# A hybrid GLA + S5 decoder block: S5 steps and gate matrix loaded beside the prologue, VectorE and ScalarE in one written order up to S5

## The chip, the core and the metric

The kernel runs on one core of a Trainium2 chip. The core has five engines that run side by side: TensorE (matrix products, PE in the profile), VectorE (DVE), ScalarE (ACT), GpSimd (POOL) and SyncE (SP, which here only issues transfers). The metric is the device time of one execution in microseconds (us); lower is better.

## The reference, cut to what matters

528 tokens (16 meta tokens and 512 of the sequence) of width 1024 go through one decoder block in fp32:

```
xn   = rmsnorm(h, g_mix_pre)
proj = xn @ w_in               # q, k, v, r, a_low, u, z_gla, z_ssm
log_a = log_sigmoid(a_low @ w_gate_up + b_gate) / 16      # decay of each GLA channel
o    = gla_chunked(q, k, v, log_a);  y_gla = (rmsnorm(o) * silu(r)) @ w_o_gla
y_s  = s5_ssm(u, ...)          # complex diagonal recurrence, 64 groups x 64 states
y_ssm = GLU(gelu(y_s) @ w_glu + b_glu)
mixed = sigmoid(z_gla) * y_gla + sigmoid(z_ssm) * y_ssm
h    = h + rmsnorm(mixed @ w_out);  h = h + rmsnorm(relu(rmsnorm(h) @ w_ff1)**2 @ w_ff2)
```

The S5 part needs, before any token is seen, a short calculation on 64 x 64 parameters: a step `exp(log_step)`, the complex factor `lam = exp(a * step)` (an exponential, a sine and a cosine), its powers 0 to 8, the eighth power normalised and its own powers (E8), and the matrices B and C scaled with these.

## The kernel before, in words

Every large product runs as three passes on a split of both operands into a high half and a rest (`mm3`, `feat_tile`): `whi` and `wlo` are the halves of a weight tile of 128 columns, `xh` and `xl` those of the normalised tokens. A weight tile is loaded to `wraw` (three buffers) on SP's queue, ScalarE makes `whi` (`split_w_hi`) and VectorE `wlo` (`split_w_lo`). One such product of 512 columns is a slot: `dense` is the list of slots, `slot()` runs one, and `fetch` splits weights two slots ahead (`AHEAD = 2`).

The kernel begins with a prologue. The first five tiles of `u` are multiplied with the unnormalised tokens (`rh`, `rl`; `raw_product`), while ScalarE squares the token rows (`squared`), `rooted` makes the reciprocal root of the mean square (`xrs`; token tiles 0 and 1 first, then 2 to 4), and `spread` and `rows_of` turn it into rows (`xrows`, `xrowp`). `scaled`, `high` and `low` then make the normalised tokens (`xT`, `xh`, `xl`) for two halves of the tokens. `u_took(..., raw=True)` takes a raw product out of PSUM into `ut`, multiplied with `xrowp`; `u_out` stores it on POOL's queue. `wa` is the split weight of the gate's low rank (`a_low`).

Then come the low-rank product (`low_rank`, result `alow`), and ten slots: three tiles of `u`, four gate tiles of z_ssm (zs0 to zs3) and three of z_gla (zg4 to zg6). Between them stand the gate products (`gate_up`, which need the split gate matrix `wgr`), the decay sums (`decay_sums`, exp, log and a scan), the S5 steps (`chain`, `powers`, `b_bar`, `chunk_powers`, `c_rows`), and the tables of S5's first block (`first`). Behind the ten slots the loop over the heads and S5's blocks begins with a product of 256 columns.

What sets the order: TensorE runs in program order through all of this (`pinned`). In the prologue VectorE and ScalarE are wrapped in `InOrder`, which keeps program order; from `V, S = nc.vector, nc.scalar` on a scheduler places their instructions. Transfers run in the order of the queue they are issued on (SP, POOL, ScalarE). In this kernel the gate matrix `wgu` is loaded with six transfers and the S5 steps and parameters `ab` with one, all on POOL's queue.

## Time and profile before

| | us |
|---|---|
| median of 3 runs | 891.54 |
| lowest and highest run | 888.96, 893.45 |
| profiled execution, its own time | 893.47 |
| its span in the profile | 891.8 |
| TensorE busy | 870.5 (98%) |
| VectorE busy | 651.7 (73%) |
| ScalarE busy | 445.6 (50%) |
| GpSimd busy | 125.3 (14%) |

The profile is one execution, with times from the start of its span. Rows name an instruction by engine, line, operation and tiles (out<-in). A row of the timeline has the start, the duration and in brackets the idle time before it and what ended that. A row of the stretches has the stretch, its length, busy time of each engine with the number of instructions, the granted TensorE clock (1.00 is full), the busy share of the transfer engines and what they moved in GB/s. With a filter for one engine only that engine's busy time is shown. In the waits a row has the waiting engine, line and tile, what it waited for, the sum, the number of times and the longest.

### The profile page before, as it was taken

To read this page: it belongs to the slowest core of one execution; us is meant where nothing else is said; L and a number is where in the kernel's file an instruction comes from. 1 tells how busy PE (TensorE), PEld (TensorE's weight loads), DVE (VectorE), ACT (ScalarE), POOL (GpSimd) and SP (SyncE) were. 2 spreads that over 40 slices of the span, in tenths; PEclk is the share of its full clock that TensorE was granted. 3 is DMA by queue.
4 is the path that set the end of the run, shared out by engine and by line. 5 is a ranking of instruction groups with operands and counts; after the bars stand their busy time and mean duration, and the time that the engine had idled before them with its cause. 6 is when DMAs were issued, how large, how long until landed. Compare 5 with 4: busy or idle time off the path is not lost.

```text
span 891.8 us, 13281 instructions
## 1 busy us (share of the span) xinstructions
PE 870.5 (98%) x4824; PEld 744.1 (83%) x4824; DVE 651.7 (73%) x1180; ACT 445.6 (50%) x751; POOL 125.3 (14%) x220
## 2 busy tenths in 40 slices
PE   9789899999999999999999999999999999999996
PEld 8778698989898888888888888988888888888885
DVE  5778979787786869966544765576667668688886
ACT  7549355676665545425333543433222236665763
POOL 0032211212122231233000000011111100000001
PEclk9979899999999999999999999999999999999999
DMA  8665775454545676667644762579998976866564
GB/s 295 200 189 138 218 233 151 124 167 116 158 113 148 157 245 167 179 193 263 196 142 146 230 179 72 190 258 307 323 322 285 336 243 222 285 199 192 168 209 142
DMA packets 167738, 180.58 MB, mean 202 GB/s; under 512 B 19096, under 2 KB 127672, under 8 KB 167672
## 3 DMA queue, kind: packets, MB, share of 16 engines
q1 hardware_dynamic: 148504, 117.43, 44.7%
q0 software_dynamic: 17856, 58.36, 19.2%
q10 hardware_dynamic: 1312, 3.94, 1.3%
q8 instruction: 38, 0.62, 0.3%
q14 instruction: 28, 0.23, 0.1%
HBM read 143.74 MB, written 35.95 MB: 202 GB/s over the span
## 4 chain that ended last, share of the span: by engine, by line
PE 90%; ACT 3%; DMA 2%; DVE 2%; issue 1%; SPq 0%; POOL 0%; DVEq 0%; ACTq 0%; POOLq 0%
PE mm L60 67%; PE sm L60 21%; PE sm L65 2%; DMA xT<-in_x_cols_dram 1%; DMA bd<-b 1%; DMA wraw<-in_w_in_dram 1%; DVE xT L78 0%; DMA ud<-ut 0%; ACT rh L78 0%; ACT xt L78 0%; DVE xl L78 0%; ACT xh L78 0%; ACT whi L160 0%; ACT whi L78 0%; DVE c L1533 0%
## 5 line engine op out<-in xcount | busy, mean ns | idle before, releaser
L160 ACT ACTIVATE whi<-wraw 128x1024 fp32r<-128x1024 f32 x99 | 104.6, 1059 | 234.6 <-PE mm L60 208.1
L175 DVE TENSOR_TENSOR wlo<-wraw,whi 128x1024 fp32r<-128x1024 f32 x99 | 121.0, 1222 | 104.1 <-ACT whi L160 103.7
L60 PE MATMUL mm<-xh,wlo 128*128 128x512 f32 (+2 forms) x464 | 158.3, 341 | 3.1 <-DVE wlo L175 3.1
L60 PE MATMUL mm<-xh,whi 128*128 128x512 f32 (+2 forms) x464 | 161.3, 348 | 0.0
L60 PE MATMUL mm<-xl,whi 128*128 128x512 f32 (+2 forms) x464 | 157.7, 340 | 0.0
L60 PE MATMUL mm<-hh,whi 128*128 128x512 f32 (+1 forms) x280 | 104.0, 371 | 0.0
L60 PE MATMUL mm<-hl,whi 128*128 128x512 f32 (+1 forms) x280 | 103.8, 371 | 0.0
L60 PE MATMUL mm<-hh,wlo 128*128 128x512 f32 (+1 forms) x280 | 103.8, 371 | 0.0
L60 PEld LDWEIGHTS mm<-xh,wlo 128*128 128x128 f32 x464 | 89.3, 192 | 12.9 <-DVE wlo L175 3.5
L60 PEld LDWEIGHTS mm<-xh,whi 128*128 128x128 f32 x464 | 89.6, 193 | 9.8 <-issue 1.2
L60 PEld LDWEIGHTS mm<-xl,whi 128*128 128x128 f32 x464 | 89.6, 193 | 8.8
L1470 DVE TENSOR_TENSOR wlo<-wraw,whi 128x1024 fp32r<-128x1024 f32 x56 | 68.4, 1222 | 19.7 <-ACT whi L1466 19.5
L60 PE MATMUL sm<-wlo,fh 128*128 128x512 f32 x192 | 74.8, 390 | 0.0
L60 PE MATMUL sm<-whi,fh 128*128 128x512 f32 x192 | 74.7, 389 | 0.0
L60 PE MATMUL sm<-whi,fl 128*128 128x512 f32 x192 | 74.7, 389 | 0.0
L1466 ACT ACTIVATE whi<-wraw 128x1024 fp32r<-128x1024 f32 x56 | 58.6, 1049 | 17.0 <-PE mm L60 11.7
L60 PEld LDWEIGHTS mm<-hh,whi 128*128 128x128 f32 x280 | 52.7, 188 | 9.1
L60 PEld LDWEIGHTS mm<-hh,wlo 128*128 128x128 f32 x280 | 52.7, 188 | 9.1
L60 PEld LDWEIGHTS mm<-hl,whi 128*128 128x128 f32 x280 | 52.7, 188 | 8.9
L160 ACT ACTIVATE fh<-f 128x512 fp32r<-128x512 f32 x48 | 30.3, 631 | 45.5 <-PE sm L60 30.4
L60 PE MATMUL mm<-gh,whi 128*128 128x512 f32 x128 | 49.8, 389 | 0.0
L60 PE MATMUL mm<-gl,whi 128*128 128x512 f32 x128 | 49.8, 389 | 0.0
(422 smaller groups left out, 1760.6 us busy)
## 6 DMA issues: line engine op xcount, KB each, us to landing
wraw<-in_w_ff_dram SPq DMA_DIRECT2D x56, 512.0 KB, 4.8
wraw<-in_w_in_dram SPq DMA_DIRECT2D x47, 512.0 KB, 4.4
w2raw<-in_w_ff_dram POOLq DMA_DIRECT2D x16, 1024.0 KB, 8.8
t2d<-w2t POOLq DMA_DIRECT2D x16, 1024.0 KB, 5.9
wraw<-t2d SPq DMA_DIRECT2D x32, 512.0 KB, 3.8
wraw<-in_w_glu_dram SPq DMA_DIRECT2D x16, 512.0 KB, 4.5
M<-kpad POOLq DMA_DIRECT2D x64, 64.0 KB, 2.7
wraw<-in_w_o_gla_dram SPq DMA_DIRECT2D x8, 512.0 KB, 6.1
```

The lines of the kernel that those rows point to most:

```text
L60: ins = nc.tensor.matmul(*args, **kw)
L65: ins = nc.tensor.transpose(*args, **kw)
L160: S.activation(dst, src, AF.Copy, scale=scale)
L175: V.tensor_sub(lo, raw, f32(hi))
L1466: halved = S.activation(bh, raw, AF.Copy)
L1470: V.tensor_sub(bl, raw, f32(bh))
```

## The change

1. **Earlier and differently queued loads.** `ab` is loaded on SP's queue in the prologue, ahead of u tile 2. The gate matrix is laid out six times over on the host's side (`w_gates`) and loaded with one transfer on SP, ahead of u tile 5, into a scratch tile that before held the causal mask's numbers. The weights of u tiles 5, 6 and 7 are loaded in the same list. The transfer of zeros to `kpad` goes from SP to POOL.
2. **One written order.** `InOrder` holds for VectorE and ScalarE until the block loop. The S5 steps are noted as a list of jobs with a cost each; `work(us)` emits jobs from the list until their costs reach `us`, and independent chains are interleaved (`in_turn`). `early_slot(before, after)` stands for `slot()` in the ten slots: it splits the weights of the slot two ahead on ScalarE, emits some jobs, then the rest of the split on VectorE, more jobs, and then the slot's own product. The decay sums are four jobs between the powers of E8. The tables of the first block are jobs, too.
3. **The raw takes.** The second halves of u tiles 0 to 4, and the first halves of 2 to 4, are taken behind `wa`, and not before the second half of the tokens is normalised. Tiles 3 and 4 get `ut` buffers of their own.
4. In the norm, the last square and the second root stand ahead of the split of u tile 3 and the casts to `xh`; ten S5 steps, the cast of the mask and two small reduces go into the prologue.
5. ScalarE's negation of `CB` is dropped, and the table subtracts where it added.

```diff
-    for kind, i in (("u", 1), ("h", 0), ("h", 4), ("u", 2), ("x", 0), ... ("u", 3), ("u", 4)):
+    for kind, i in (("u", 1), ("h", 0), ("h", 4), ("a", 0), ("u", 2), ("x", 0), ... ("u", 3), ("u", 4), ("w", 0), ("g", 0), ("u", 5), ("c", 0), ("u", 6), ("u", 7)):
...
+            elif kind == "a":
+                loaded = nc.sync.dma_start(ab, io["a_step"])
...
+            elif kind == "g":
+                wgu = scratch()[:96].rearrange("p a b -> p (a b)")
+                loaded = nc.sync.dma_start(wgu, io["w_gates"])
...
+    V.tensor_copy(tri, trif)
+    work(1.6)
     squared(2)
...
     squared(3)
+    squared(4)
     scaled(0, range(0, 4))
+    rooted(slice(2, TT + 1))
     w3 = split_w(raws[3])
-    squared(4)
+    scaled(0, range(4, 8))
     high(0, range(0, 4))
-    rooted(slice(2, TT + 1))
...
-    for i in range(2):
-        u_took(last[i], uts[i], 1, True)
-        u_out(i, uts[i])
...
+    late_take(0, 1)
+    late_take(1, 1)
+    f0 = split_w(raws[5])
+    late_take(2, 0)
+    late_take(2, 1)
+    late_take(3, 0)
+    late_take(3, 1)
+    f1_hi = split_w_hi(raws[6])
+    late_take(4, 0)
+    f1 = f1_hi, split_w_lo(raws[6], f1_hi)
+    late_take(4, 1)
...
+    def work(us):
+        while jobs and us > 0:
+            cost, op = jobs.pop(0)
+            op()
+            us -= cost
...
+    def early_slot(before, after):
+        n = at[0]
+        at[0] += 1
+        raw = raws[7] if n == 0 else raw_w(dense[n + AHEAD][0])[1]
+        hi = split_w_hi(raw)
+        for go in (before, after):
+            if callable(go):
+                go()
+            else:
+                work(go)
+            if hi is not None:
+                ready[n + AHEAD] = hi, split_w_lo(raw, hi)
+                hi = None
+        dense[n][1](ready.pop(n))
...
+    early_slot(1.0, 3.6)
     gate_up(0)
     gate_up(1)
-    for _ in range(2):
-        next(steps, None)
-    slot()
+    early_slot(2.5, 2.2)
     gate_up(2)
     gate_up(3)
...
+    early_slot(2.5, 2.2)
+    early_slot(2.2, decay_logs)
+    work(2.4)
+    early_slot(2.2, c_rows)
+    work(2.4)
+    early_slot(2.5, 2.2)
+    early_slot(2.2, 100.0)
```

How rows move on VectorE, in three places. First, the second half of the norm in the prologue. Before (`mm_254`, `mm_255`, `mm_324`, `mm_379` are the banks of raw u products):

```order
L78 TENSOR_TENSOR ut_149<-mm_254,xrowp_148 128x8x32
L78 TENSOR_TENSOR ut_150<-mm_255,xrowp_148 128x8x32
L78 TENSOR_TENSOR ut_151<-mm_324,xrowp_148 128x8x32
L78 TENSOR_TENSOR ut_151<-mm_379,xrowp_148 128x8x32
L78 TENSOR_TENSOR ut_505<-mm_324,xrowp_148 128x8x32
L78 SCALAR_TENSOR_TENSOR xT_110<-xT_110,g_10_108,xrows_147 128x272 x4
L78 TENSOR_TENSOR xl_98<-xT_110,xh_97 128x2x272 x2
L78 TENSOR_TENSOR wa_553<-waraw_141,wa_553 128x8x16
```

Now:

```order
L79 TENSOR_TENSOR wlo_508<-wraw_179,whi_499 128x1024
L79 TENSOR_TENSOR xl_101<-xT_149,xh_100 128x2x256 x2
L79 SCALAR_TENSOR_TENSOR xT_149<-xT_149,g_44_147,xrows_198 128x272 x4
L79 TENSOR_TENSOR xl_101<-xT_149,xh_100 128x2x272 x2
L79 TENSOR_TENSOR wa_607<-waraw_181,wa_607 128x8x16
L79 TENSOR_TENSOR ut_203<-mm_310,xrowp_199 128x8x32
L79 TENSOR_TENSOR ut_204<-mm_311,xrowp_199 128x8x32
L79 TENSOR_TENSOR wlo_618<-wraw_185,whi_616 128x1024
```

The takes into `ut` have gone from ahead of the second half's `xT` and `xl` to behind `wa`, with the split of u tile 5 (`wlo_618`) between them. (Rows of the same kind between those shown are left out in both.)

Second, the gate matrix, behind the low-rank product. Before (`wlo_639` and `wlo_835` belong to u tile 7 and to zs0):

```order
L175 TENSOR_TENSOR wlo_639<-wraw_635,whi_637 128x1024
L508 TENSOR_TENSOR alow_582<-mm_643,alow_582 32x256
L508 TENSOR_TENSOR alow_582<-mm_663,alow_582 32x272
L633 TENSOR_SCALAR ab_611<-ab_611 128x64
L726 TENSOR_TENSOR den_911<-ab_611 128x64
L175 TENSOR_TENSOR wlo_835<-wraw_831,whi_833 128x1024
L498 TENSOR_TENSOR wgr_581<-wgu_574,wgr_581 32x512
L637 SCALAR_TENSOR_TENSOR edr_684<-edk_683,ab_611 128x64
```

Now (`wlo_631` and `wlo_713` belong to u tiles 6 and 7):

```order
L79 TENSOR_TENSOR wlo_631<-wraw_190,whi_628 128x1024
L79 TENSOR_TENSOR ut_72_207<-sm_582,xrowp_199 128x8x32
L79 TENSOR_TENSOR alow_641<-mm_663,alow_641 32x256
L79 TENSOR_TENSOR alow_641<-mm_683,alow_641 32x272
L79 TENSOR_TENSOR wgr_640<-sc_60_183,wgr_640 32x512
L79 SCALAR_TENSOR_TENSOR ede_138<-ede_138,edr_137 128x64 x6
L79 TENSOR_TENSOR wlo_713<-wraw_192,whi_705 128x1024
```

The split of the gate matrix now stands right behind `alow`, and the first S5 step, which reads `ab`, no longer stands ahead of it.

Third, the weights of gate tile zg4. Before (`b_179`, `b_180` are the decay sums of heads 2 and 3, `E_79_597` is E8):

```order
L533 SCALAR_TENSOR_TENSOR b_179_1171<-mn_584,ga_583 128x16
L533 SCALAR_TENSOR_TENSOR b_180_1178<-mn_584,ga_583 128x128
L235 TENSOR_TENSOR mta_1149<-E_79_597 128x512
L236 TENSOR_TENSOR epb_1150<-E_79_597 128x512
L533 SCALAR_TENSOR_TENSOR b_180_1178<-mn_584,ga_583 128x16
L175 TENSOR_TENSOR wlo_1189<-wraw_1185,whi_1187 128x1024
L1033 TENSOR_TENSOR M_196_1249<-CA_592,Lr_590 128x8x128
```

Now (`b_187` is the sum of head 3):

```order
L79 SCALAR_TENSOR_TENSOR b_179_1167<-mn_643,ga_642 128x128 x4
L79 SCALAR_TENSOR_TENSOR b_179_1167<-mn_643,ga_642 128x16
L79 TENSOR_TENSOR wlo_1174<-wraw_1157,whi_1159 128x1024
L79 TENSOR_TENSOR mta_1176<-E_16_113 128x512
L79 TENSOR_TENSOR epb_1177<-E_16_113 128x512
L79 SCALAR_TENSOR_TENSOR b_187_1214<-mn_643,ga_642 128x128 x4
L79 TENSOR_TENSOR wlo_1221<-wraw_1210,whi_1212 128x1024
```

The low half of zg4's weights (`wlo_1189`, now `wlo_1174`) has come ahead of the last powers of E8 and of the fourth decay sum.

## The prediction

> **What bounds the kernel now.** I read the page first, then the busy time by stretches, then TensorE's waits, then the timelines of the engines it waits for. The page's head, TensorE's line and its granted clock in 40 slices:

> ```profile
> span 891.8 us, 13281 instructions
> ...
> PEclk9979899999999999999999999999999999999999
> ```

> Clock and work dip only in the first five slices. The stretches (TensorE's busy time is the second number, the granted clock the last decimal before the DMA share):

> ```profile
> 120.00:880.00 760.00, 760.00 (x4189) 646.62 (x4188) 552.42 (x886) 372.71 (x610) 100.88 (x172) 1.00 0.65 203
> 880.00:892.00 12.00, 4.05 (x18) 3.00 (x17) 5.29 (x14) 1.97 (x6) 1.05 (x2) 0.83 0.29 88
> ```

> From 120 us to 880 us TensorE never waits and runs at full clock, so what the first 119 us lose or gain reaches the end undiminished. Who TensorE waited for up to 170 us (us, times, longest), and the clock after those waits:

> ```profile
> PE mm L60 <- DVE wa L78: 4.4, 1, 4.4
> PE mm L60 <- DVE wlo L175: 3.1, 1, 3.1
> PE sm L60 <- DVE wgr L498: 3.0, 1, 3.0
> PE sm L60 <- DVE xrs L78: 1.5, 1, 1.5
> ```

> ```profile
> 27.30:30.00 2.70, 2.62 (x20) 2.47 (x21) 2.70 (x7) 2.25 (x8) 0.00 (x0) 1.00 1.07 357
> 44.50:48.50 4.00, 4.00 (x21) 3.01 (x22) 3.83 (x10) 2.70 (x5) 3.23 (x5) 0.57 0.61 163
> 59.00:66.00 7.00, 7.00 (x34) 7.00 (x35) 6.66 (x46) 3.46 (x9) 0.00 (x0) 0.54 0.39 116
> 100.10:106.60 6.50, 6.45 (x16) 5.04 (x17) 6.50 (x8) 1.57 (x4) 1.57 (x3) 0.52 0.83 204
> ```

> Four waits, all for VectorE. After each of the three long ones the clock is near a half for 4 to 7 us; after the 1.5 us one it is not. Where they lie on TensorE:

> ```profile
> 39.81 0.28 PE L60 MATMUL sm<-rh,wlo 128*128 128x272 f32 x1
> 44.50 0.28 PE L60 MATMUL mm<-xh,wa 128*32 128x256 f32 x1 [4.40 <-DVE wa L78]
> 49.91 0.28 PE L60 MATMUL mm<-xh,whi 128*128 128x256 f32 x1
> 59.00 1.25 PE L60 MATMUL sm<-alow,wgr 96*128 96x256 f32 x4 [3.04 <-DVE wgr L498]
> 100.15 0.79 PE L60 MATMUL mm<-xh,wlo 128*128 128x512 f32 x1 [3.09 <-DVE wlo L175]
> 118.85 0.39 PE L60 MATMUL mm<-xh,wlo 128*128 128x512 f32 x1
> 119.08 0.28 PE L60 MATMUL mm<-xh,whi 128*128 128x256 f32 x1
> ```

> The product that begins at 119.08 is the first of the heads; TensorE's order up to it is the same in both kernels. (49.91 is where u tile 5 begins behind the low-rank product.) What can be won is the waits, 4.40 + 3.04 + 3.09 + 1.46 = 11.99 us, and the clock, 4.0 x 0.43 + 7.0 x 0.46 + 6.5 x 0.48 = 1.72 + 3.22 + 3.12 = 8.06 us: 20.05 us, with that product at 119.1 - 20.0 = 99.0.

> **The change part by part.** *The second root.* ScalarE's rows:

> ```profile
> 20.93 1.06 ACT L78 ACTIVATE xt<-xt 128x1024 f32<-128x1024 f32 x1
> 23.01 1.06 ACT L78 ACTIVATE whi<-wraw 128x1024 fp32r<-128x1024 f32 x1 [0.93 <-DMA wraw<-in_w_in_dram]
> 23.98 1.04 ACT L78 ACTIVATE xt<-xt 16x1024 f32<-16x1024 f32 x1
> 26.23 0.29 ACT L78 ACTIVATE xra<-xss,epst 128x3 f32<-128x3 f32 x1
> ```

> ```profile
> 27.16 0.16 DVE L78 SCALAR_TENSOR_TENSOR xrs<-xra,xrs 128x3 f32<-128x3 f32 x1
> ```

> The last square now precedes the split of u tile 3, and the root the casts to xh: 20.93 + 2 x 1.15 + 0.3 = 23.5 instead of 26.52. VectorE's steps behind the root took until 27.32, 0.8 us, so xrs is there at 24.3. TensorE wants it at 25.9. The 1.46 goes. The step table on SP's queue ahead of u tile 2 is 96 KB and pushes the transfers behind it by some 0.3 us at the 357 GB/s quoted above; the only one awaited there is u tile 3, whose split now comes 0.4 us later anyway.

> *The raw takes behind the gate weights.* VectorE's rows:

> ```profile
> 27.24 1.67 DVE L78 SCALAR_TENSOR_TENSOR xT<-xT,g,xrows 128x256 f32<-128x256 f32 x4
> 28.82 1.29 DVE L78 TENSOR_TENSOR xl<-xT,xh 128x512 fp32r<-128x512 f32 x2
> 30.97 1.23 DVE L78 TENSOR_TENSOR wlo<-wraw,whi 128x1024 fp32r<-128x1024 f32 x1 [0.86 <-ACT whi L78]
> 33.32 1.66 DVE L78 TENSOR_TENSOR ut<-mm,xrowp 128x256 f32<-128x256 f32 x7
> 37.89 0.42 DVE L78 TENSOR_TENSOR ut<-mm,xrowp 128x256 f32<-128x256 f32 x1 [2.92 <-DMA ud<-ut]
> 38.24 1.73 DVE L78 SCALAR_TENSOR_TENSOR xT<-xT,g,xrows 128x272 f32<-128x272 f32 x4
> 44.08 0.28 DVE L78 TENSOR_TENSOR wa<-waraw,wa 128x128 fp32r<-128x128 f32 x1
> ```

> Before, the second half of the tokens (38.24 to 44.36, 6.1 us) stood behind 2.1 us of takes and a 2.92 us wait for a store of ut. Now from 24.3 come two wlo (2.4), four xT (1.7) and four xl (2.6): 31.0, then the 6.1: wa at 37.1. TensorE ends the raw products at 40.1 - 1.5 = 38.6. What is late next is the PSUM bank of the low-rank product, which needs the first take behind wa (0.5 us): 37.6. The 4.40 goes, and its 1.72 of clock; the takes' new tiles have their own buffers, so the 2.92 goes too.

> *The gate matrix and the step table.* Before, six loads of the gate matrix and the step table sat on POOL behind the stores of ut:

> ```profile
> 48.78 2.52 POOL L491 DMA_DIRECT2D wgu<-in_w_gate_up_dram  x5
> 51.29 0.58 POOL L629 DMA_DIRECT2D ab<-in_a_step_dram  x1
> ```

> ```profile
> 56.24 0.20 DVE L633 TENSOR_SCALAR ab<-ab 128x64 f32<-128x64 f32 x1 [4.76 <-DMA ab<-in_a_step_dram]
> 58.26 0.68 DVE L498 TENSOR_TENSOR wgr<-wgu,wgr 32x512 fp32r<-32x512 f32 x1
> 59.72 1.26 DVE L651 SCALAR_TENSOR_TENSOR ede<-ede,edr 128x64 f32<-128x64 f32 x5
> 98.89 1.20 DVE L175 TENSOR_TENSOR wlo<-wraw,whi 128x1024 fp32r<-128x1024 f32 x1
> ```

> Now one 192 KB load goes out on SP ahead of u tile 5. Behind wa VectorE has thirteen takes (some 3.4 us by the row of seven), two wlo (2.4), two alow (0.8, an estimate from the takes) and wgr (0.7): 37.1 + 7.3 = 44.4. TensorE needs wgr after the low-rank product (44.50 to 49.9 before, at full clock 5.4 - 1.7 = 3.7) and u tile 5 (49.91 to the wait's start at 55.96, 6.0): 38.6 + 9.7 = 48.3. Slack 3.9; the 3.04 and its 3.22 go. The load adds a wait: its tile is the mask's scratch tile, so SP's queue, with u tiles 5 to 7 and the C columns behind it, stands until VectorE has cast the mask, right behind the first root, at some 19.3. Before, SP reached that place only now:

> ```profile
> 19.59 1.67 SPq L328 DMA_DIRECT2D waraw<-in_w_in_dram  x1
> ```

> So it costs nothing. The clearing of that tile on POOL waits for wgr (44.4), and behind it the store of u tile 5, which is due at 48.3: nothing. The zeros of kpad move from SP to POOL, behind the stores of ut; their readers come after 125 us, nothing waits.

> *One written order up to S5.* The 3.09 us wait was for the low half at 98.89, the weights of gate tile zg4; VectorE was simply behind. Its busy time from the end of wa to the low half of the product at 119.08, and its S5 steps interleaved:

> ```profile
> 44.36:111.55 67.19, 56.64 (x191) 0.87 0.64 181
> 62.00:68.00 6.00, 5.97 (x48) 0.72 0.07 21
> ```

> Of 67.19 us 56.64 are work. The changed order does that work less some 2.8 (ten steps at about 0.2 moved into the norm, the mask's cast and two reduces ahead of it), and more 2.1 of takes (the rows at 33.32 and 37.89) and 1.5 for a table product of block 1 (128x1024, 1.2 like a wlo, and small ones): 57.4, so 37.1 + 57.4 = 94.5, against a need at 99.0. That is the lower end of its lateness, 4.5 us early. The upper end: five steps that wait for each other take 1.26 (0.25 each), 48 interleaved ones 5.97 (0.124), and some 40 steps of the new order have a neighbour they wait for: 40 x 0.126 = 5.0, so 99.5, or 0.5 late; ScalarE's copies ahead of E can add half a microsecond. I take 1.0 us lost for all ten slots together, near the late end, because every slot must hold on its own; less than nothing is excluded, since a wait that is gone can't shrink further. The dropped negation of CB, 1 us of ScalarE, the zeroing of E and the six loads fewer on POOL lie on engines that are not late: nothing.

> The sum against the profiled execution, 893.47 us (1.7 outside the span): 893.47 - 20.05 + 1.0 = 874.4. It lay 1.9 above the median of the runs, 891.54; on that the same 19 us give **872.5**.

> [...]

> **The rivals.** *A, VectorE becomes the bound in the gate slots.* The margin at 99.0 runs from 4.5 early to 1 late. If all of the steps, some 87, went at 0.25, they would take 11.0 more, less 4.5: 6.5 us late, 878.0 with no drop of clock, 881.2 with one. The trace speaks against it (48 in 5.97); 5% on 57 us, 2.9 late and one drop of 3.2, gives 877.6, and is the likelier form. [...]

> *B, given back in the first block.* VectorE was 7.5 us ahead at 119.08 and is about even now. If its decays and tables come 3 us late and the clock drops once (3.2), 878.7. Against: it has 1.2 us less to do there, since one table product is already made. Chance 0.10.

> *C, lockstep, slower.* With ScalarE and VectorE held to one order, the split of the weights two slots on stands behind copies that wait for TensorE's own product. If in each of the ten slots it begins only when the product before ends, TensorE waits 1.06 + 1.14 = 2.2 us in each: 22 us, 893.5; and from waits of 3 us, where the clock drops, 1.7 more in each, 910. It decides from the point where a split starts over 3 us after its place. For: ScalarE's strict place behind the sigmoid. Against: the split is two products ahead, and a product of 24 passes at 0.23 (118.85 to 119.08), 5.5 us, covers 2.2. Chance 0.05.

> *D, it doesn't do what it says:* waits of 3 us with their clock (6.2 together) merely move to other slots: two give 883.9, three 890.1. Chance 0.03.

> **How the numbers follow.** Forecast 0.65, A 0.17, B 0.10, C 0.05, D 0.03. The range reaches from all 20.05 won on the lowest run (889.0 - 20.0, 868.9, and a little for the run) to A's far end: 868 to 882. It leaves out C, D and the tails. A measurement of this kernel tells about 0.5%, 4.5 us, from no change: faster is forecast, A, B and half of D, 0.93; same 0.03; slower 0.04.

> **What would show it.** Right: no wait of TensorE for wa, wgr, xrs or the low half of zg4, a granted clock of 1.00 from 10 us on, the heads' first product near 99 to 100, TensorE full from there, VectorE over 90% busy from 31 us to there. Wrong: a wait for wlo above 1.5 us, clock at 0.5 anywhere behind 10 us, ScalarE waiting for TensorE ahead of a split (C), or a wait for e_gk or a table in the first block (B).

## The result, and the profile after

The median of four runs is 880.33 us (879.85 to 881.0) against 891.82 (888.96 to 893.45) for four runs of the kernel before: ratio 0.9875, 95% interval 0.9849 to 0.9902. The profiled execution took 881.0 us, 12.5 less than that of before. So the change is faster, by 1.25%, and inside the forecast's range, but of the 19 us forecast on the median only 11.5 came.

The page's head and clock, and the waits of TensorE up to 170 us (us, times, longest) in the kernel after:

```profile
span 879.3 us, 13267 instructions
...
PEclk9999899999999999999999999999999999999998
```

```profile
PE mm L61 <- DVE wlo L79: 3.2, 1, 3.2
PE sm L61 <- DVE xss L507: 1.3, 1, 1.3
PE sm L66 <- DVE e_gk L977: 1.1, 1, 1.1
PE mm L61 <- ACT whi L79: 0.9, 2, 0.6
```

The waits for wa, wgr, xrs and the low half of zg4 are gone (xss is the start of the program, as before). Two new ones stand there: 3.2 us for a low half and 1.1 us for e_gk. TensorE's timeline has the same marks as before: the first product with wa, the first with wgr, the new wait, the first of the heads, and the wait in the first block:

```profile
38.54 0.28 PE L61 MATMUL mm<-xh,wa 128*32 128x256 f32 x1
48.24 0.65 PE L61 MATMUL sm<-alow,wgr 96*128 96x256 f32 x4
97.52 0.80 PE L61 MATMUL mm<-xh,wlo 128*128 128x512 f32 x1 [3.25 <-DVE wlo L79]
105.27 0.28 PE L61 MATMUL mm<-xh,whi 128*128 128x256 f32 x1
133.28 0.62 PE L66 MATMUL sm<-ident,e_gk 128*16 128x128 f32 x4 [1.05 <-DVE e_gk L977]
```

TensorE runs the same products in the same order in both, so each start can be set against the same one before. The difference is the ledger of the change:

| first product of | before | after | difference | step in it |
|---|---|---|---|---|
| u tile 0, second half | 13.70 | 14.03 | +0.33 | start of the program |
| the products behind the second root | 28.34 | 26.95 | -1.39 | xrs: -1.7 |
| u tile 5 (behind wa) | 49.91 | 42.35 | -7.56 | wa and its clock: -6.2 |
| the first gate tile | 74.65 | 60.98 | -13.67 | wgr and its clock: -6.1 |
| the heads | 119.08 | 105.27 | -13.81 | gate slots: -0.1 |
| the next gate tile, behind the wait for e_gk | 146.23 | 133.66 | -12.57 | e_gk: +1.2 |

The first three terms came as forecast, 14 us. The gate slots, where another 5.2 were expected, gave 0.1: the old wait of 3.09 us with its half clock was replaced by a new one of 3.25 with its own. Between the two, TensorE led by 19.9 us (a product that started at 106.29 now started at 86.40). The stretches show the clock (the last decimal before the DMA share) and VectorE (the fourth number, its busy time):

```profile
37.80:88.60 50.80, 50.80 (x314) 45.49 (x313) 48.01 (x174) 35.74 (x65) 15.84 (x27) 1.00 0.68 202
88.60:93.90 5.30, 5.30 (x26) 4.35 (x24) 0.10 (x1) 2.16 (x5) 0.88 (x2) 1.00 1.04 293
96.40:103.10 6.70, 5.58 (x13) 4.42 (x14) 6.60 (x8) 1.06 (x1) 0.00 (x0) 0.50 0.69 208
```

VectorE works 48.0 of 50.8 us and then stands for 5.3, with the DMA engines full (1.04) at that time. Its timeline there, and the issues on SP and GpSimd that belong to it:

```profile
87.28 1.21 DVE L79 TENSOR_TENSOR BA<-BA,prm 128x1024 f32<-128x1024 f32 x1
88.42 0.28 DVE L237 TENSOR_TENSOR epb<-E 128x128 f32<-128x128 f32 x1
93.97 1.22 DVE L79 TENSOR_TENSOR M<-M,prm 128x1024 f32<-128x1024 f32 x1 [5.27 <-DMA B<-bard]
95.11 1.22 DVE L1088 TENSOR_TENSOR M<-CA,Lr 128x1024 f32<-128x1024 f32 x1
96.25 1.22 DVE L79 TENSOR_TENSOR wlo<-wraw,whi 128x1024 fp32r<-128x1024 f32 x1
...
103.57 1.22 DVE L79 TENSOR_TENSOR wlo<-wraw,whi 128x1024 fp32r<-128x1024 f32 x1
```

```profile
83.06 0.64 POOL L1075 DMA_DIRECT2D B<-bard  x1
83.47 0.54 SPq L1245 DMA_DIRECT2D M<-in_b_cols_dram  x1
```

```profile
wraw<-in_w_in_dram SPq DMA_DIRECT2D x11, 512.0 KB, 3.8
B<-bard POOLq DMA_DIRECT2D x1, 512.0 KB, 11.0
M<-in_b_cols_dram SPq DMA_DIRECT2D x1, 512.0 KB
```

Here the releaser must be read with care. The row at 93.97 names the transfer B<-bard, but that product does not read B, and B landed 11.0 us after its issue, at 94.06, when the product had begun. What it reads is the other half of b_cols (the tile that the code calls `other`; the trace calls its space M). That transfer has no landing of its own in the table; the last of the 16 updates of its semaphore in the trace is at 93.85. It took 10.4 us, where 512 KB of weights take 3.8 in the median. The low half of the last gate slot's weights, zg6 (the row at 96.25), stands behind it in the written order. (The row at 103.57 is the low half of the first head's weights.)

The same two steps in the kernel before:

```profile
90.56 0.34 SPq L805 DMA_DIRECT2D M<-in_b_cols_dram  x1
102.88 1.22 DVE L808 TENSOR_TENSOR M<-M,prm 128x1024 f32<-128x1024 f32 x1
```

Before, the product came 12.3 us behind the issue. The change brought the product's turn forward by 14.2 us (102.88 to 88.70) and the issue by 7.1 (90.56 to 83.47), since the load still stands on SP behind weights whose buffers come free only as the slots go by. The loss was made by a load that was not moved with its reader.

### The profile page after: what moved, and what is told of

Read it like the earlier page. It is cut to its first block, busy times and chain, and to the rows that moved or that the text cites. A ratio compares the mean times of both kernels' runs of the same rounds, so it can differ in the third digit from the quotient of the medians.

```text
span 879.3 us, 13267 instructions
## 1 busy us (share of the span) xinstructions
PE 864.8 (98%) x4824; PEld 739.0 (84%) x4824; DVE 653.0 (74%) x1180; ACT 442.7 (50%) x749; POOL 121.8 (14%) x214
## 3 DMA queue, kind: packets, MB, share of 16 engines
q0 software_dynamic: 17744, 58.52, 19.9%
## 4 chain that ended last, share of the span: by engine, by line
PE 92%; DMA 3%; DVE 2%; ACT 2%; SPq 1%; issue 1%; DVEq 0%; POOL 0%
PE mm L61 68%; PE sm L61 23%; PE sm L66 2%; DMA B<-bard 1%; DMA U<-ud 1%; DMA wraw<-in_w_in_dram 1%; ACT ga L79 0%; SPq L1110 0%; DVE b L79 0%; ACT whi L79 0%; ACT L79 0%; DVE c L1596 0%; SPq L467 0%; DVE wlo L79 0%; ACT prm L79 0%
## 5 line engine op out<-in xcount | busy, mean ns | idle before, releaser
L161 ACT ACTIVATE whi<-wraw 128x1024 fp32r<-128x1024 f32 x87 | 92.2, 1059 | 217.0 <-PE mm L61 191.8
L176 DVE TENSOR_TENSOR wlo<-wraw,whi 128x1024 fp32r<-128x1024 f32 x87 | 106.3, 1222 | 103.5 <-ACT whi L161 103.2
L1533 DVE TENSOR_TENSOR wlo<-wraw,whi 128x1024 fp32r<-128x1024 f32 x56 | 68.4, 1222 | 22.4 <-ACT whi L1529 22.1
L1529 ACT ACTIVATE whi<-wraw 128x1024 fp32r<-128x1024 f32 x56 | 58.7, 1049 | 19.2 <-PE mm L61 11.7
```

Of the source, the lines that this page charges most:

```text
L161: S.activation(dst, src, AF.Copy, scale=scale)
L176: V.tensor_sub(lo, raw, f32(hi))
L1529: halved = S.activation(bh, raw, AF.Copy)
L1533: V.tensor_sub(bl, raw, f32(bh))
```

## The experiments

Each has four to six runs. The first four experiments ran on one chip and the second four on another; the kernel before had a median of 892.02 us on the first and 891.41 on the second.

**The table first.** Theory L: one late transfer at the head of VectorE's list makes the loss. Theory W: VectorE has too much work in these slots.

```
 jobs.append((1.2, lambda: V.tensor_mul(BA, BA, fr)))
+jobs.extend((c, lambda: next(first, None)) for c in (2.6, 1.4))
 jobs.append((1.2, lambda: V.tensor_mul(other, other, fi)))
 jobs.append((1.2, lambda: V.tensor_add(BA, BA, other)))
-jobs.extend((c, lambda: next(first, None)) for c in (2.6, 1.4, 1.2, 2.6))
+jobs.extend((c, lambda: next(first, None)) for c in (1.2, 2.6))
```

> One part changed in the kernel after: VectorE's written jobs, so that the first block's table products (which need nothing new) stand ahead of the product with the late half of b_cols. Theory L (one late transfer at the head of VectorE's list): VectorE stood idle 5.27 us at 88.70 for that half, landed at 93.85; with the table first the weights of the last gate slot are ready at about 92.3, ahead of TensorE's 94.27, so the 3.25 us wait goes, and with it the half clock from 96.4 to 103.2 (about 2.4 us): 5.65 less, 880.3 -> 874.7. Rival W (VectorE has too much work in these slots): the low half is late anyway, 880 within 0.5. Rival G (given back): the same 5.65 go here, but the first block's wait for e_gk, 1.05 us now, grows by 2 to 3 us as TensorE comes 5.65 earlier: 876.7 to 877.7.

Measured: 875.69 us (875.43 to 877.79), ratio to before 0.9823 (0.9801 to 0.9845); 4.6 less than after. VectorE's timeline: the same work, in another order, without a pause, and the low half of zg6 done at 93.2, where TensorE comes at 94.2:

```profile
88.29 1.22 DVE L79 TENSOR_TENSOR M<-CA,Lr 128x1024 f32<-128x1024 f32 x1
...
91.96 1.22 DVE L79 TENSOR_TENSOR wlo<-wraw,whi 128x1024 fp32r<-128x1024 f32 x1
```

What is left on TensorE is the wait in the first block, grown from 1.05:

```profile
PE sm L66 <- DVE e_gk L977: 1.8, 1, 1.8
```

W falls. L holds for the slots, and in this execution 0.7 us of G, the give-back, is there too. Two of the five runs, 877.52 and 877.79, lie 2 us above the other three and inside G's range; no trace of these two was kept.

**The half loaded early.** The other way to take the late transfer away:

```
-other = mk(b5, [P, GB, P], tag="M3", bufs=1)...
-nc.sync.dma_start(other..., io["b_cols"][1])
+others = [mk(pq, ..., tag="q"), mk(pq, ..., tag="qt")]   # beside BA, 32 groups each
 ...
     loaded = nc.sync.dma_start(dst..., src)               # CA, CB, BA, as before
+    for i, o in enumerate(others):
+        loaded = nc.sync.dma_start(o..., io["b_cols"][1][:, 512 * i : 512 * i + 512])
```

> One part changed in the kernel after: the other half of b_cols is loaded early, behind the first half on SP (two 256 KB pieces in tiles of its own), so it is there before VectorE asks; two products and two sums of half the size take the place of one each (0.3 us more of VectorE). Theory L: as with the table first, 874.7, and 512 KB less in the crowded 11 us from 83 on, so that the block's B lands before 94.0. Rival W: 880 within 0.5. Rival G: 876.7 to 877.7. If the 512 KB in the early crowd make the raw u weights late, a wait for whi between 25 and 45 us shows it.

Measured: 873.85 us (873.47 to 874.01), ratio 0.9792 (0.9769 to 0.9815): the fastest of all kernels here, 18 us under before and 6.5 under after. Its page and its stretches:

```profile
span 872.3 us, 13268 instructions
...
PE   9999999999999999999999999999999999999996
```

```profile
10.00:120.00 110.00, 109.43 (x760) 101.15 (x760) 102.48 (x286) 73.05 (x140) 22.62 (x39) 1.00 0.80 239
120.00:860.00 740.00, 740.00 (x4018) 627.12 (x4017) 538.91 (x865) 361.04 (x589) 95.54 (x162) 1.00 0.66 204
```

TensorE misses 0.6 us of the 850 after the tenth, all at full clock; the heads' first product starts at 99.43. B, issued at 83.4 as before, landed at 90.8 instead of 94.06, and the wait for e_gk is gone without an edit to it.

**B behind the half.** Why did the transfer take 10.4 us? Theory C: it shared the DMA engines with B.

```
-blocks[0].loads(nc.gpsimd)
 first = blocks[0].tables()
 other = ...
 nc.sync.dma_start(other..., io["b_cols"][1])
+blocks[0].loads()          # on SP
```

> One part changed in the kernel after: the first block's B and lam are issued on SP behind the other half of b_cols, instead of on GpSimd's queue 0.4 us ahead of it. Theory C (the half took 10.4 us to land, where 512 KB of weights take 3.8 in the median, because it shared the DMA engines with B): it lands at about 88, VectorE does not wait, 874.7. Rival Q (it is late whatever goes with it, by its issue at 83.47 and the scattered U transfers): it lands at 92 or later, 879 to 880.5. What may spoil the gain: weights behind B and lam on SP come 2 to 4 us later, a wait for whi in the first block.

Measured: 875.2 us (875.06 to 875.55), ratio 0.981 (0.979 to 0.983). VectorE's row:

```profile
89.27 1.23 DVE L79 TENSOR_TENSOR M<-M,prm 128x1024 f32<-128x1024 f32 x1 [0.55 <-DMA M<-in_b_cols_dram]
```

Issued at 83.34, the half now landed at 89.24: 5.9 us instead of 10.4, a little over the 88 expected, and the wait shrank from 5.27 to 0.55. C holds: most of the lateness was B beside it. What made up the rest, 5.9 against 3.8, stays open. With B beside it on GpSimd's queue the half on SP's queue took 4.5 us more (10.4 less 5.9).

**wa behind the takes.** One part undone: do the terms of the sum add up?

```
-S.activation(wa[:, :, :16], wraw, AF.Copy)
-V.tensor_sub(wa[:, :, 16:], wraw, f32(wa)[:, :, :16])
 late_take(0, 1)
 ...
 late_take(4, 1)
+S.activation(wa[:, :, :16], wraw, AF.Copy)
+V.tensor_sub(wa[:, :, 16:], wraw, f32(wa)[:, :, :16])
```

> One part undone in the kernel after: wa's copy and difference stand behind all raw takes again. By the sum of the prediction TensorE waits 4.4 us for wa and runs at half clock for 1.7 us more; if the terms add, 880.3 + 6.1 = 886.4. Rival S (the slots absorb it: VectorE was waiting for a transfer in slot zg6, and TensorE's 3.25 us wait there shrinks as TensorE comes later): 880.5 to 883.

Measured: 886.53 us (884.94 to 887.48), ratio 0.9934 (0.9914 to 0.9954): 6.2 more than after. In the medians the terms add; S, the absorption, falls, because the issue of the half on SP moved along with the slots (83.47 to 89.4). That it fits to 0.1 us is in part luck, since in the profiled execution the slots lost their time in another way than in the kernel after, as the stretches below show. TensorE's waits:

```profile
PE mm L61 <- DVE wlo L79: 4.9, 2, 3.1
PE mm L61 <- DVE wa L79: 4.3, 1, 4.3
```

The stretches of this run held a surprise. The wait of 3.13 us at zg6, from 100.20 to 103.33, did not lower the clock, and one of 1.76 us behind it, from 108.89 to 110.66, did (TensorE's busy time is the second number):

```profile
98.50:101.80 3.30, 1.70 (x8) 1.08 (x6) 2.02 (x2) 0.60 (x1) 0.56 (x1) 1.00 1.00 305
101.90:105.20 3.30, 1.86 (x8) 1.54 (x9) 3.30 (x4) 0.17 (x1) 0.00 (x0) 1.00 0.74 217
105.30:108.60 3.30, 3.30 (x16) 2.73 (x15) 3.20 (x6) 0.79 (x1) 0.00 (x0) 1.00 0.73 189
108.70:112.00 3.30, 1.54 (x13) 1.35 (x12) 3.30 (x5) 1.57 (x2) 0.54 (x1) 1.00 0.41 152
112.10:115.40 3.30, 3.30 (x18) 3.30 (x17) 3.27 (x8) 0.73 (x2) 0.00 (x0) 0.50 0.59 183
```

These five are cut in steps of 3.41 us counted from the trace's own changes of clock (47.22, 112.07 and 115.48 in this run: 19 such steps and one). The long wait was shared by two stretches, each over half busy; the short one lay in one. So the last runs were made on the fastest kernel, where nothing else waits.

**The price of a wait.** The low half of the first head's weights is computed again once, twice or three times (k):

```
 ready[n + AHEAD] = hi, split_w_lo(raw, hi)
+for _ in range(k if n == 8 else 0):
+    V.tensor_sub(ready[n + AHEAD][1], raw, f32(hi))
```

> On the kernel of half_loaded_early (873.85 us, runs 0.54 apart, TensorE never waits behind 10 us): the low half of the first head's weights is computed twice on VectorE (1.14 us more in front of TensorE's 100.05, slack 0.2). What a wait costs, by its length. Theory I (a wait of 3 us or more halves the clock, a shorter one costs its length): wait 0.9 to 1.3, 874.8 to 875.2, runs within 0.6. Theory P (the clock is set in stretches of 3.41 us whose phase is free; a stretch idle for about half or more is followed by one at half clock): the same, since no stretch can be idle for 1.7 us.

> As late_by_one, with the low half computed three times: a wait of 2.1 to 2.7 us. Theory I: it costs its length, 876.0 to 876.6, runs within 0.6. Theory P: in some runs the wait falls into one stretch and the next 3.41 us run at half clock, in others not: runs in two or three groups, some at 876.0 to 876.6 and some 1.7 or 3 us above, the median 876 to 878.5, spread 1.5 or more.

> As late_by_one, with the low half computed four times: a wait of 3.2 to 4.0 us. Theory I: always the same price, the wait and 2.4 to 3.1 us of clock, 879.5 to 880.9 within 0.6. Theory P: the wait and either one stretch at half clock (1.7 us, when the wait ends ahead of the stretch or early in it) or two (3 us), seldom none: 878.7 to 880.9 in groups, spread 1.2 or more.

| k | wait in the profiled run | runs, us | above 873.85 |
|---|---|---|---|
| 1 | 1.44 | 874.77, 875.02, 875.40, 875.75, 876.57 | 0.9 to 2.7 |
| 2 | 2.71 | 876.51, 876.94, 877.99, 878.06 | 2.7 to 4.2 |
| 3 | 3.99 | 878.79, 878.87, 879.79, 880.25 | 4.9 to 6.4 |

(873.85 was measured on the other chip, where the kernel before took 0.6 us more; the last column can be off by that much.) The profiled runs of k = 2 and k = 3, their stretches cut at the steps of 3.41 us:

```profile
97.70:101.10 3.40, 1.71 (x9) 1.27 (x7) 3.40 (x6) 1.66 (x3) 0.54 (x1) 1.00 0.87 246
101.20:104.50 3.30, 2.39 (x20) 2.39 (x21) 3.30 (x6) 2.96 (x4) 0.00 (x0) 1.00 0.54 164
```

```profile
98.30:101.60 3.30, 0.95 (x6) 0.62 (x4) 3.30 (x5) 1.64 (x2) 0.54 (x1) 1.00 0.63 216
101.70:108.50 6.80, 5.26 (x24) 5.26 (x25) 6.80 (x11) 2.10 (x4) 0.00 (x0) 0.50 0.40 111
```

A wait of 2.71 us fell on both sides of a step and cost its length, 876.51; two other runs of the same kernel took 1.5 more, at a mean clock of 0.995 instead of 0.997 and 0.999 (the fast kernel without the wait has 0.997 to 0.999). That fits theory P; theory I, one price by length, gives no two groups. With k = 3 there are two groups again: 878.8 and 878.9 at a mean clock of 0.997, 879.8 and 880.3 at 0.993 and 0.994. With k = 1 the runs are 1.8 apart where both theories said 0.6, at an equal clock: P explains the clock and not all of the spread, and where the rest of it came from stays open. (0.5 us of it lies outside the program's span: the longest run, 876.57, is 2.3 us longer than its span, the others 1.8.)

**The second root late.** The first term alone, on the same fast kernel:

```
 squared(3)
-squared(4)
 scaled(0, range(0, 4))
-rooted(slice(2, TT + 1))
 w3 = split_w(raws[3])
-scaled(0, range(4, 8))
+squared(4)
 high(0, range(0, 4))
+rooted(slice(2, TT + 1))
+scaled(0, range(4, 8))
```

> On the kernel of half_loaded_early, one part undone: the second root of the norm stands behind the next split and the high halves again. By the sum TensorE waits 1.46 us for xrs at 26 and nothing else: 873.85 + 1.5 = 875.3; by theory P one wait of 1.5 us is below half a stretch, so the clock stays at 1.00 and the runs within 0.6. Rival S (absorbed, because VectorE's list is what sets the end of the gate slots): 873.9 to 874.3.

Measured: 877.3 us (875.61 to 878.0), 3.4 above the fast kernel, more than either case expected. The stretches around the wait, 26.25 to 28.13:

```profile
25.80:29.10 3.30, 1.43 (x11) 1.06 (x9) 2.05 (x9) 3.02 (x9) 0.00 (x0) 1.00 1.05 322
29.20:32.50 3.30, 3.30 (x16) 3.30 (x17) 3.30 (x6) 1.53 (x6) 0.00 (x0) 0.50 1.02 402
```

The wait was 1.87 us, all in one stretch, and the next ran at half clock: 1.9 + 1.6. Three of the four runs took 877.2 to 878.0 and one 875.61, at a higher mean clock (0.998 against 0.996). The expectation of a wait of 1.46 us at full clock failed: the wait was longer, and 1.87 us in one stretch did not keep the clock.

## Why the prediction was right, and where it was not

*What bounds the kernel: right.* TensorE's starts from 146 us on keep their distance to those of before, 12.6 us there and 12.4 at the end. What the first 134 us gained is the gain.

*The second root, the raw takes and the gate matrix: right.* xrs was there at 24.45 (24.3 forecast), wa at 37.02 (37.1), wgr at 44.69 (44.4). The terms were 1.46, 6.12 and 6.26; the ledger has 1.7, 6.2 and 6.1. Undoing the second costs 6.2; undoing the first costs 3.4 on the fast kernel, where its wait took a stretch of clock along, which it did not in the kernel before. The third rests on the ledger alone, since no run undoes it. One sum is off without harm: thirteen takes by the row of seven are 3.1 us, and not 3.4 (they took 3.4). No wait for the PSUM bank showed (38.54 against 38.6). The SP wait for the mask's cast and the new order on GpSimd's queue cost nothing that shows.

*One written order up to S5: here the sum failed.* "I take 1.0 us lost for all ten slots together" was to stand for VectorE's own speed, with the bounds set by its work, 57.4 us, and by its dependent steps: the low half for the heads ready between 94.5 and 99.5. Where no transfer is late, in half_loaded_early (with 0.3 us more work for VectorE), it was ready at 99.87, just past the late bound:

```profile
98.65 1.22 DVE L79 TENSOR_TENSOR wlo<-wraw,whi 128x1024 fp32r<-128x1024 f32 x1
```

So choosing a value near the late end was right for VectorE's speed. Interleaved steps stayed short:

```profile
47.88:52.21 4.33, 4.30 (x33) 1.00 1.03 336
```

That is 0.131 us each (0.124 forecast), where those that wait for each other took 0.25 (five in 1.26 us, in the kernel before). VectorE had reached the product with the late half at 88.70, and tables_first shows that the work fits. What the term left out is a wait of VectorE itself: the load of the other half, which keeps its place on SP while its reader moves forward. It cost 5.27 us on VectorE and, in the profiled execution, 3.25 of waiting and 2.8 of clock on TensorE (22 products from 97.52 to 105.27 take 7.75 us, 4.99 at 0.2267 each). So 6.0 in place of 1.0. The prediction followed the loads that the diff moves, and not one whose reader it moves.

The 2.8 of clock are not a price on top of the wait. VectorE worked without a pause behind 93.97 and had the low half for the heads at 104.79 (the row at 103.57); without the drop TensorE would have asked for it at 102.7 and waited some 2 us there (an estimate: 105.5, its third product of the heads, less 2.8). That is what happened with wa late, where the clock held at zg6 and the next wait, 1.76 us, was for that low half. It fits the four runs of the kernel after: their mean clock is 0.993 (the profiled one), 0.997, 0.995 and 0.997, and their times lie within 1.15 us. So VectorE's lateness would have cost nearly as much at full clock; only the profiled one of the four was traced, so for the others this is argued, not shown.

*The rivals.* Of A the sign came, a wait for wlo above 1.5 us, but not its mechanism: VectorE was idle, not overloaded, though with the load gone it had little to spare (99.87, and TensorE took that half at 99.92). B came in small: 1.05 us for e_gk, without a drop of clock. Ahead of it VectorE's low half had waited for ScalarE, and that for weights from the same crowded stretch:

```profile
122.01 1.06 ACT L161 ACTIVATE whi<-wraw 128x1024 fp32r<-128x1024 f32 x1 [4.86 <-DMA wraw<-in_w_in_dram]
123.10 1.23 DVE L176 TENSOR_TENSOR wlo<-wraw,whi 128x1024 fp32r<-128x1024 f32 x1 [2.92 <-ACT whi L161]
```

The wait for e_gk is gone in the two kernels whose transfers were thinned or reordered, and there in the one where they were not; that the crowd made it is argued from this, not shown by itself. C did not come; its 1.7 us of clock in each wait of 3 us is what the wait of 4.40 showed, while behind 3.04 and 3.09 the kernel before lost 3.2 and 3.1. D came once (a wait of 3 us that moved to another slot), not twice. The forecast of 872.5 is 1.35 us from what the change gives when the one load goes along, 873.85.

*The number: inside the range, in part by luck.* Three of the prediction's own signs of being wrong came: a wait for wlo of 3.25 us, a clock of 0.5 behind 10 us and a wait for e_gk; and the heads began at 105.27, not near 99 to 100. 880.33 lies below 882 because that end of the range had been set for A, which is not what happened.

*The clock.* The 8.06 us of clock were read from one execution as if they belonged to the waits. They are partly chance, as the last section has it, though the 18.2 us that the fast kernel gains lie nearer to the 19 of that reading than to the 16.1 that the same sum gives with one stretch of 3.41 us at half clock for each long wait (11.99 + 3 x 1.71 - 1.0, an estimate). The kernel before has runs from 889.81 to 895.06 in the first four experiments, the fast kernel without waits from 873.47 to 874.01.

## What to carry to other kernels

When a change moves work forward on an engine, list what each moved step reads and find the issue of each of those loads: a load that keeps its place becomes the new wait, and in an in-order list everything behind it, here the weights that TensorE needs, pays for it. Put steps whose inputs are there ahead of steps whose inputs are in flight, or send the load along with its reader. And where a row names a releaser that the waiting step doesn't read, look for the transfer that it does read.

## What the runs showed of the hardware

```profile
125.90:129.20 3.30, 1.54 (x11) 1.20 (x9) 3.30 (x6) 3.29 (x8) 0.00 (x0) 1.00 0.60 183
129.30:132.70 3.40, 3.40 (x17) 2.80 (x16) 3.30 (x11) 0.85 (x3) 0.00 (x0) 1.00 0.64 179
```

Where a stretch at half clock began with a remainder of the wait, 0.42 us for wgr and 0.61 for zg4 in the kernel before, 1.16 in the kernel after and some 1.6 with k = 3, a second one followed. Where the wait had ended ahead of it, 0.43 us for wa in the kernel before, 1.41 with wa late (the wait of 1.76) and some 1.0 with the second root late, none did. In the kernel before, the half clock behind the 4.40 us for wa, which ended at 44.50, lasted from 44.93 to 48.34, and that behind the 3.04 for wgr, which ended at 59.00, from 58.58 to 65.41:

```profile
45.00:48.30 3.30, 3.30 (x18) 2.41 (x16) 3.30 (x8) 2.00 (x5) 3.03 (x5) 0.50 0.71 191
58.60:65.40 6.80, 6.40 (x30) 6.41 (x31) 6.42 (x43) 3.08 (x8) 0.07 (x1) 0.50 0.40 119
```

So 3.25 us went with 6.8 us at half clock in the kernel after and 4.40 us with only 3.4 in the kernel before, and no wait here had a fixed price. In the profiled executions it was, up to some 1.5 us, its length at full clock, and from there to 4.4 us its length and 0, 1.6 to 1.7 or 2.6 to 3.2 us more, by where it fell. What makes the clock drop these rows alone do not show: of two stretches with 1.54 us of work one was followed by half clock and one was not.
